# The start of a two-block transformer kernel reordered: smaller first loads, two norms on GpSimd, the context last

## The chip, the cores and the metric

The kernel runs on one core of one Trainium2 chip. The metric is the device time of one execution in microseconds (us). Before the change it is 849.24 us, the median of 3 runs (847.86 to 849.66). The engines are TensorE (PE, with its weight loads as PEld), VectorE (DVE), ScalarE (ACT), GpSimd (POOL) and SyncE (SP), which issues all the DMAs here. Each engine works through its own instructions in a fixed order, and waits on semaphores for the others.

## The reference

The reference runs a first block on `x` (256 tokens of 1024 columns) with a context `ctx` of 256 tokens, and then a second block with a memory `mem` of 256 tokens. What the change touches lies at the first block's start, and in the part of the second block that needs only `mem`:

```python
mod = jax.nn.silu(c) @ w_ada[l] + b_ada[l]            # c: the condition; 6 x 1024 columns
sh1, sc1, gt1, sh2, sc2, gt2 = jnp.split(mod[:, None, :], 6, axis=-1)
mod_c = jax.nn.silu(c_ctx) @ w_ada[l] + b_ada[l]
...
h = modulate(rmsnorm(x, g_norm1[l]), sh1, sc1)         # h * (1 + scale) + shift
hc = modulate(rmsnorm(ctx, g_norm1[l]), shc1, scc1)
cq, ckv, kpe, rq, rk, rv, rg = split_proj(h @ w_in[l])
cq_c, ckv_c, kpe_c, rq_c, rk_c, rv_c, rg_c = split_proj(hc @ w_in[l])
...
m = rms_norm(mem, g_mem[l])                            # second block, cross attention
k = (m @ wk).reshape(B, M, XATTN_HEADS, XATTN_HEAD_DIM)
v = (m @ wv).reshape(B, M, XATTN_HEADS, XATTN_HEAD_DIM)
```

## The kernel before

**Precision.** A weight or an activation is split into a high and a low part in a rounded 32-bit format: ACT makes the high part (`wh`, `xTh`), DVE subtracts it from the source and gets the low part (`wl`, `xTl`). A product is then three matmuls: high by high, high by low, low by high (`mm3`, L185; for the keys of `mem`, `k_step`, L394). So each 512 KB block of weights (a unit) costs one load into one of 7 `raw` buffers, two ACT instructions (L229 where a gain is multiplied in, L222 where not), two DVE instructions (L230, L225) and 12 or 24 matmuls. A `raw` buffer is free again when DVE has read it.

**The start.** `mem`, `x` and `ctx` come transposed (`memT`, `xnT`, `cnT`; `load_T`, L302). `mem_steps` is a list of 16 steps, one unit each: 8 of the keys (`wk_x`, 24 matmuls of 256 columns) and 8 of the values (`wv_x`, 12 matmuls of 512 columns). The modulation rows of the first block need `w_ada`, whose first 2048 columns are 16 loads of 512 KB, used unsplit straight from `raw` (`ada_unit`, L328, 4 matmuls each, into 32-row strips). A string sets in which order the program writes them:

```python
START = 'mmaamxXmaammaammaamaamaakmaaacaC'   # L36
```

Here `m` is a mem step, `a` a unit of `w_ada`, `x` and `c` the loads of `x` and `ctx`, `X` and `C` their norms, `k` a load of constants. After the second `m` the norm of `mem` is written. 11 mem steps stand in the string, the other 5 after the modulation of `x`.

**A norm** (`token_rms`, L354 to L375) squares the transposed tensor on ACT (L357, two instructions of 1024 columns), folds it on DVE (L359, L360, L362: 1024, 512 and 256 columns), sums over partitions with two matmuls against ones (L365), copies the sums to SBUF on DVE (L367), takes the power -0.5 on POOL (L138, L139), spreads the result over the diagonal on DVE (L372) and broadcasts it with one matmul (L374). For `x` and `ctx`, DVE then multiplies (L427).

**After the start.** When the 16 units of `w_ada` are done, `ada_fm` (L343) makes shift and scale, `mod_split` (L468, L471, L159, L160) applies them to `x`, the 5 left mem steps run, and the first projection of `x` begins (four units of `w_in` of 512 columns, 48 matmuls, called the c projection here). The second projection needs `ctx` modulated too (`at<-wh,xTh` are its matmuls on `ctx`).

**What sets the order.** The program is written for a tile framework whose scheduler moves instructions within each engine by priorities (`hp`, `prio`) and by its own costs; the result is one fixed list for each engine. At most 8 DMAs are under way, and a load into `raw` waits for the buffer's last reader.

Of the kernel before, what the change touches and what calls it, by code (L numbers as in the profile page):

```python
# [9 lines left out]
F32 = mybir.dt.float32  # L10
# [4 lines left out]
ALU = mybir.AluOpType  # L15
# [17 lines left out]
MID = 1  # L33
GPU = 3
GPN = 16
START = 'mmaamxXmaammaammaamaamaakmaaacaC'  # L36
NT2 = 3
NS1 = 4
ZORD = ('ka', 'qa', 'qh', 'gh', 'fh', 'ih')
# [50 lines left out]
def _body(nc, tc, A, out, es):  # L90
# [197 lines left out]
    with ExitStack() as e1:  # L288
# [9 lines left out]
        nc.vector.memset(silc, 0.0)  # L298
        C1 = lambda n: c1[:, CST[n][0] - 128:CST[n][1] - 128]

        def load_T(dst, name, q):
            nc.sync.dma_start(dst[:, 4 * q:4 * q + 4, :],  # L302
                              A[name][:, q * 1024:(q + 1) * 1024].rearrange("p (k n) -> p k n", k=4))

        memT = S8()
        wk_units = [units_for(W, A["wk_x"], g * 512, 512, 8, "g_mem") for g in range(2)]
        memT_h = S8(dt=F32R)
        memT_l = S8(dt=F32R)
        load_T(memT, "memT", 0)
        nc.sync.dma_start(fm, A["fm"])  # L310
        for u in wk_units[0][0:HEAD]:
            u.load()
        load_T(memT, "memT", 1)
        nc.sync.dma_start(ident, A["cst1"][:, 0:128])
        for q in range(2):
            ks = slice(4 * q, 4 * q + 4)
            split_from(memT_h[:, ks, :], memT_l[:, ks, :], memT[:, ks, :])
            if q == 0:
                for u in wk_units[0][0:HEADS]:
                    u.get()  # L320
        nc.scalar.activation(silc[:, :, 0:2].rearrange("p k s -> p s k"), fm[:, 0:16].rearrange("p (s k) -> p s k", s=2),
                             AF.Silu)
# [28 lines left out]
        rmem = []  # L351
        rmb = S1()

        def token_rms(xT):  # L354
            sq = [S4() for _ in range(2)]
            for q in range(2):
                nc.scalar.activation(sq[q].rearrange("p (k n) -> p k n", k=4), xT[:, 4 * q:4 * q + 4, :], AF.Square,  # L357
                                     scale=D ** -0.5)
            nc.vector.tensor_tensor(out=sq[0], in0=sq[0], in1=sq[1], op=ALU.add)  # L359
            nc.vector.tensor_tensor(out=sq[0][:, 0:512], in0=sq[0][:, 0:512], in1=sq[0][:, 512:1024], op=ALU.add)  # L360
            s1 = S1()
            nc.vector.tensor_tensor(out=s1, in0=sq[0][:, 0:256], in1=sq[0][:, 256:512], op=ALU.add)  # L362
            t = tr_tile()
            for i in range(2):
                nc.tensor.matmul(t[:, i:i + 1], lhsT=s1[:, i * P:(i + 1) * P], rhs=ones[:, 0:1], start=True, stop=True)  # L365
            ss = small(2, "ss")
            nc.vector.tensor_copy(ss, t[:, 0:2])  # L367
            r = finish_rstd(ss, 2)
            d = S1()
            t = tr_tile()  # L370
            for i in range(2):
                nc.vector.tensor_scalar(out=d[:, i * P:(i + 1) * P], in0=ident, scalar1=r[:, i:i + 1], scalar2=None,  # L372
                                        op0=ALU.mult)
            nc.tensor.matmul(t[:, 0:T], lhsT=ones, rhs=d, start=True, stop=True)  # L374
            return r, t[:, 0:T]  # L375
# [8 lines left out]
        for g in range(2):  # L384
# [17 lines left out]
                                                in1=rmb.unsqueeze(1).broadcast_to([P, 2, T]), op=ALU.mult)  # L402
            for i, u in enumerate(wk_units[g]):
                mem_steps.append(lambda u=u, i=i, f=k_step: f(u, i))
        for g in range(2):
            st = {}

            def v_step(u, i, g=g, st=st):
                if i == 0:
                    st["acc"] = [acc_tile(), acc_tile()]  # L410
                for t in range(2):
                    sl = slice(t * P, (t + 1) * P)
                    gemm_unit([st["acc"][t]], (memT_h[:, :, sl], memT_l[:, :, sl]), u, 8)
                    if i == 3:
                        nc.scalar.activation(vm[t][:, g * 512:(g + 1) * 512], st["acc"][t], AF.Copy, scale=rmem[t])
            for i, u in enumerate(units_for(W, A["wv_x"], g * 512, 512, 8, "g_mem")):
                mem_steps.append(lambda u=u, i=i, f=v_step: f(u, i))

        xnT = S8()
        cnT = S8()  # L420

        @prio("nt")
        def norm_T(dst):
            r, rb = token_rms(dst)
            for q in range(2):
                ks = slice(4 * q, 4 * q + 4)
                nc.vector.tensor_tensor(out=dst[:, ks, :], in0=dst[:, ks, :],  # L427
                                        in1=rb.unsqueeze(1).broadcast_to([P, 4, T]), op=ALU.mult)

        n_mem = n_ada = 0  # L430
        for ch in START:
# [7 lines left out]
                n_ada += 1  # L439
            elif ch == "x":  # L440
                for q in range(2):
                    load_T(xnT, "xT", q)
            elif ch == "c":
                for q in range(2):
                    load_T(cnT, "ctxT", q)
            elif ch == "k":
                nc.sync.dma_start(c1, A["cst1"][:, 128:NC1])
            elif ch == "X":
                norm_T(xnT)
            elif ch == "C":  # L450
# [1079 lines left out]
```

## Time and profile before

| what | value |
|---|---|
| median of the timed runs | 849.24 us |
| the profiled execution | 849.74 us |
| its span (first to last instruction) | 848.0 us |
| PE busy | 815.4 us, 96% |
| DVE busy | 587.6 us, 69% |
| ACT busy | 453.7 us, 54% |
| POOL busy | 50.3 us, 6% |

Times below are counted from the span's start. A busy share is an average over stages; PE's idle time is what is left of the span. In a timeline a row is a run of like instructions: its start, how long it lasted, engine, line, what it writes and reads, how often, and in brackets how long the engine stood idle before it and what ended that. The matmuls' ends are modelled and overlap, so the pace is read from the starts of rows that follow each other.

### The profile page before, as it was taken

How to read it: one execution, taken by the hardware profiler on the slowest of the kernel's cores; microseconds unless marked ns; L12 is line 12 of the kernel's file. 1: busy time of each engine (PE TensorE's matmuls, PEld its weight loads, DVE VectorE, ACT ScalarE, POOL GpSimd, SP SyncE). 2: the span in 40 equal slices, each digit the busy share in tenths (PEclk: the TensorE clock that was granted, in tenths of full speed). 3: DMA queues.
4: the chain of work that ended last, by engine and by line, in shares of the span. 5: the costliest groups of instructions: out<-in, count | busy, mean ns of one | idle time of the engine just before them, and what ended most of it. 6: DMA issues, size and time to landing. Idle time of an engine off the chain costs nothing.

```text
span 848.0 us, 12889 instructions
## 1 busy us (share of the span) xinstructions
PE 815.4 (96%) x4944; PEld 689.1 (81%) x4944; DVE 587.6 (69%) x900; ACT 453.7 (54%) x717; POOL 50.3 (6%) x85
## 2 busy tenths in 40 slices
PE   6989989999999999999999999999999999999996
PEld 5857967666787899999997877777788899999995
DVE  5649879985787697667577767776747855656642
ACT  7348364234556675555455757665626845544531
POOL 0000020111010000000002200101001100000000
PEclk9999999999999999999999999999999999999999
DMA  9797869762155566565664643343624676666501
GB/s 338 271 356 283 280 236 341 253 225 75 50 162 177 188 209 197 176 197 178 196 178 146 184 139 110 138 126 124 198 75 126 196 223 183 190 182 192 176 1 51
DMA packets 65150, 155.27 MB, mean 183 GB/s; under 512 B 5184, under 2 KB 10816, under 8 KB 65088
## 3 DMA queue, kind: packets, MB, share of 16 engines
q1 hardware_dynamic: 65088, 154.44, 56.8%
q8 instruction: 39, 0.64, 0.3%
q14 instruction: 23, 0.19, 0.1%
HBM read 152.85 MB, written 1.05 MB: 181 GB/s over the span
## 4 chain that ended last, share of the span: by engine, by line
PE 67%; ACT 3%; DVE 2%; issue 1%; POOL 1%; DVEq 0%; POOLq 0%; ACTq 0%
PE acc L185 32%; PE at L255 12%; PE tr L255 12%; PE tr L167 1%; PE at L1293 1%; PE at L1271 1%; PE tr L1212 1%; ACT xh L222 1%; DVE xl L225 1%; ACT junk L143 1%; PE at L1162 1%; PE at L1164 1%; PE tr L756 0%; PE at L785 0%; PE at L802 0%
## 5 line engine op out<-in xcount | busy, mean ns | idle before, releaser
L222 ACT CAST wh<-raw 128x1024 fp32r<-128x1024 f32 (+1 forms) x90 | 91.0, 1013 | 103.6 <-PE acc L185 29.4
L225 DVE TENSOR_TENSOR wl<-raw,wh 128x1024 fp32r<-128x1024 f32 (+1 forms) x87 | 104.2, 1200 | 47.5 <-ACT wh L222 46.8
L225 DVE TENSOR_TENSOR xl<-raw,xh 128x1024 fp32r<-128x1024 f32 x68 | 84.4, 1245 | 42.3 <-ACT xh L222 41.9
L185 PE MATMUL acc<-wh,xTh 128*128 128x512 f32 (+2 forms) x272 | 99.8, 392 | 0.3 <-ACT xTh L159 0.3
L222 ACT CAST xh<-raw 128x1024 fp32r<-128x1024 f32 x68 | 70.8, 1047 | 53.5 <-PE tr L255 24.6
L185 PE MATMUL acc<-wl,xTh 128*128 128x512 f32 (+2 forms) x272 | 97.8, 384 | 0.0
L185 PE MATMUL acc<-wh,xTl 128*128 128x512 f32 (+2 forms) x272 | 97.6, 383 | 0.0
L229 ACT ACTIVATE wh<-raw,fm 128x512 fp32r<-128x512 f32 (+3 forms) x96 | 64.0, 712 | 50.7 <-issue 15.6
L230 DVE SCALAR_TENSOR_TENSOR wl<-raw,fm,wh 128x512 fp32r<-128x512 f32 (+3 forms) x96 | 67.2, 742 | 25.6 <-ACT wh L229 25.3
L185 PEld LDWEIGHTS acc<-wh,xTh 128*128 128x128 f32 x272 | 50.6, 190 | 12.2 <-issue 2.1
L185 PEld LDWEIGHTS acc<-wl,xTh 128*128 128x128 f32 x272 | 50.5, 189 | 10.1 <-issue 2.0
L185 PEld LDWEIGHTS acc<-wh,xTl 128*128 128x128 f32 x272 | 50.6, 189 | 9.9 <-issue 1.5
L185 PE MATMUL acc<-xh,xTl 128*128 128x512 f32 x144 | 53.5, 397 | 0.0
L185 PE MATMUL acc<-xl,xTh 128*128 128x512 f32 x144 | 53.3, 396 | 0.2 <-DVE xl L225 0.2
L185 PE MATMUL acc<-xh,xTh 128*128 128x512 f32 x144 | 53.1, 396 | 0.0
L230 DVE SCALAR_TENSOR_TENSOR xl<-raw,fm,xh 128x512 fp32r<-128x512 f32 (+1 forms) x44 | 33.3, 796 | 17.8 <-ACT xh L229 17.7
L185 PE MATMUL acc<-xh,g 128*128 128x512 f32 x160 | 44.5, 391 | 0.0
L229 ACT ACTIVATE xh<-raw,fm 128x512 fp32r<-128x512 f32 (+1 forms) x44 | 31.1, 756 | 22.5 <-issue 13.0
L539 DVE SCALAR_TENSOR_TENSOR g<-raw,silc,g 128x1024 f32<-128x1024 f32 x28 | 36.8, 1313 | 0.1
L185 PE MATMUL acc<-wh,g 128*128 128x512 f32 x128 | 36.3, 390 | 0.0
L185 PEld LDWEIGHTS acc<-xh,g 128*128 128x128 f32 x160 | 29.6, 188 | 5.8
L185 PEld LDWEIGHTS acc<-xl,xTh 128*128 128x128 f32 x144 | 26.7, 188 | 6.4 <-DVE xl L225 1.1
(381 smaller groups left out, 1736.1 us busy)
## 6 DMA issues: line engine op xcount, KB each, us to landing
raw<-in_w_up_dram SPq DMA_DIRECT2D x66, 512.0 KB, 3.8
raw<-in_w_ada_dram SPq DMA_DIRECT2D x48, 512.0 KB, 5.6
raw<-in_w_down_dram SPq DMA_DIRECT2D x44, 512.0 KB, 3.6
raw<-in_w_in_dram SPq DMA_DIRECT2D x38, 512.0 KB, 4.0
raw<-in_w_gate_dram SPq DMA_DIRECT2D x22, 512.0 KB, 3.7
raw<-in_w_out_dram SPq DMA_DIRECT2D x16, 512.0 KB, 3.5
raw<-in_wk_x_dram SPq DMA_DIRECT2D x8, 512.0 KB, 5.8
raw<-in_wv_x_dram SPq DMA_DIRECT2D x8, 512.0 KB, 8.2
```

The costliest lines, as they stand in the source:

```text
L143: nc.scalar.activation(junk[:, 0:a.shape[-1]], a, AF.Square, scale=n ** -0.5, accum_out=ss)
L167: nc.tensor.transpose(t[:, j * P:(j + 1) * P], src[:, (b + j) * P:(b + j + 1) * P], ident)
L185: nc.tensor.matmul(accs[i], lhsT=xl if f == 2 else xh, rhs=wl[i] if f == 1 else wh[i], start=first and f == 0, stop=last and f == 2)
L222: nc.scalar.copy(wh[:, 0:n], raw[:, 0:n])
L225: eng.tensor_tensor(out=wl[:, 0:n], in0=raw[:, 0:n], in1=wh[:, 0:n].bitcast(F32), op=ALU.subtract)
L229: nc.scalar.activation(wh[:, s], raw[:, s], AF.Copy, scale=gains[k])
L230: nc.vector.scalar_tensor_tensor(out=wl[:, s], in0=raw[:, s], scalar=gains[k], in1=wh[:, s].bitcast(F32), op0=ALU.mult, op1=ALU.subtract)
L255: nc.tensor.matmul(accs[b // 2][:, (b % 2) * T:(b % 2 + 1) * T], lhsT=wt[:, o:o + P], rhs=xt[:, k, :], start=k == 0 and fl == 0 and b % 2 ...
L539: nc.vector.scalar_tensor_tensor(out=ada_cur[g], in0=raw, scalar=silc[:, k, 0:1], in1=ada_cur[g], op0=ALU.mult, op1=ALU.add)
L1162: nc.tensor.matmul(o[cs, hs], lhsT=ATs[cs, cols], rhs=ih[cs, hs], start=True, stop=cg == 0)
L1164: nc.tensor.matmul(o[cs, hs], lhsT=qi[:, cols], rhs=Sst[cg - 1][:, hs], start=False, stop=True)
L1212: nc.tensor.matmul(sc[:, j * nk:(j + 1) * nk], lhsT=qTs[pr_, hd * P:(hd + 1) * P], rhs=kTs[pr_, 0:nk], start=True, stop=True)
```

## The change

- `fm`, a tensor of small columns with the condition in it, is loaded first, and the Silu of the condition is ACT's first work. The first half of `memT` and the first unit of `wk_x` are loaded in two pieces each, alternately; `memT` is split in three pieces.
- The norms of `mem` and `x` are squared and folded on POOL (`early=True`). The norm of `ctx` squares on ACT and folds on DVE as before. The factor 1/1024 moves from the squares to the copy of the sums.
- `START` has 12 mem steps ahead of the last units of `w_ada` (11 before; 4 are left for after the modulation), and the norm of `x` has priority there. `L` loads the units of `wv_x` that are left, and then `ctx`; the norm of `ctx` is written after the last mem step.
- The two columns `lb0`, `lb1` of the second block get a load of their own, late.

```diff
-START = 'mmaamxXmaammaammaamaamaakmaaacaC'
+START = 'mmaamxXaammaamaammaamkaammaamaaL'
...
-        def load_T(dst, name, q):
-            nc.sync.dma_start(dst[:, 4 * q:4 * q + 4, :],
-                              A[name][:, q * 1024:(q + 1) * 1024].rearrange("p (k n) -> p k n", k=4))
+        def load_T(dst, name, k0, nk=4):
+            nc.sync.dma_start(dst[:, k0:k0 + nk, :],
+                              A[name][:, k0 * T:(k0 + nk) * T].rearrange("p (k n) -> p k n", k=nk))
...
-        load_T(memT, "memT", 0)
         nc.sync.dma_start(fm, A["fm"])
-        for u in wk_units[0][0:HEAD]:
-            u.load()
-        load_T(memT, "memT", 1)
-        nc.sync.dma_start(ident, A["cst1"][:, 0:128])
-        for q in range(2):
-            ks = slice(4 * q, 4 * q + 4)
-            split_from(memT_h[:, ks, :], memT_l[:, ks, :], memT[:, ks, :])
-            if q == 0:
-                for u in wk_units[0][0:HEADS]:
-                    u.get()
         nc.scalar.activation(silc[:, :, 0:2].rearrange("p k s -> p s k"), fm[:, 0:16].rearrange("p (s k) -> p s k", s=2),
                              AF.Silu)
+        u0 = wk_units[0][0]
+        u0.raw = W().raw()
+        for k in range(2):
+            load_T(memT, "memT", 2 * k, 2)
+            nc.sync.dma_start(u0.raw[:, k * 512:(k + 1) * 512], u0.ap[k * P:(k + 1) * P, :])
+        load_T(memT, "memT", 4)
+        wk_units[0][1].load()
+        nc.sync.dma_start(ident, A["cst1"][:, 0:128])
+        for k0, nk in ((0, 2), (2, 2), (4, 4)):
+            ks = slice(k0, k0 + nk)
+            split_from(memT_h[:, ks, :], memT_l[:, ks, :], memT[:, ks, :])
+            if k0 == 0:
+                u0.get()
+            if k0 == 2:
+                wk_units[0][1].get()
...
-        def token_rms(xT):
+        def token_rms(xT, early=True):
             sq = [S4() for _ in range(2)]
+            eng = nc.gpsimd if early else nc.vector
             for q in range(2):
-                nc.scalar.activation(sq[q].rearrange("p (k n) -> p k n", k=4), xT[:, 4 * q:4 * q + 4, :], AF.Square,
-                                     scale=D ** -0.5)
-            nc.vector.tensor_tensor(out=sq[0], in0=sq[0], in1=sq[1], op=ALU.add)
-            nc.vector.tensor_tensor(out=sq[0][:, 0:512], in0=sq[0][:, 0:512], in1=sq[0][:, 512:1024], op=ALU.add)
+                xq = xT[:, 4 * q:4 * q + 4, :]
+                sv = sq[q].rearrange("p (k n) -> p k n", k=4)
+                if early:
+                    nc.gpsimd.tensor_tensor(out=sv, in0=xq, in1=xq, op=ALU.mult)
+                else:
+                    nc.scalar.activation(sv, xq, AF.Square)
+            eng.tensor_tensor(out=sq[0], in0=sq[0], in1=sq[1], op=ALU.add)
+            eng.tensor_tensor(out=sq[0][:, 0:512], in0=sq[0][:, 0:512], in1=sq[0][:, 512:1024], op=ALU.add)
             s1 = S1()
-            nc.vector.tensor_tensor(out=s1, in0=sq[0][:, 0:256], in1=sq[0][:, 256:512], op=ALU.add)
+            eng.tensor_tensor(out=s1, in0=sq[0][:, 0:256], in1=sq[0][:, 256:512], op=ALU.add)
...
-            nc.vector.tensor_copy(ss, t[:, 0:2])
+            nc.vector.tensor_scalar(out=ss, in0=t[:, 0:2], scalar1=1.0 / D, scalar2=None, op0=ALU.mult)
...
-            elif ch == "c":
+            elif ch == "L":
+                for i in range(n_mem, 16):
+                    wv_units[(i - 8) // 4][i % 4].load()
                 for q in range(2):
-                    load_T(cnT, "ctxT", q)
+                    load_T(cnT, "ctxT", 4 * q)
...
             elif ch == "X":
-                norm_T(xnT)
-            elif ch == "C":
-                norm_T(cnT)
+                with hp("nt"):
+                    norm_T(xnT)
...
             mem_steps[i]()
+        norm_T(cnT, False)
```

The scheduler puts the moved work into each engine's list. First POOL, from its first norm on. In the names here and below, `s_94` is `memT`, `s_95` and `s_96` are its high and low part, `s_125` (before) or `s_129` (after) is `xnT`, `s_126` or `s_130` is `cnT`, and `g_181`, `g_182`, `g_251`, `g_252` are squares. Before:

```order
L138 TENSOR_SCALAR rs_190<-ss_188 128x2 [waits DVE_49]
L139 TENSOR_TENSOR rs_190<-rs_190,mhalf 128x2 [waits Pool_49]
L138 TENSOR_SCALAR rs_260<-ss_258 128x2 [waits DVE_49]
L139 TENSOR_TENSOR rs_260<-rs_260,mhalf 128x2 [waits Pool_49]
L138 TENSOR_SCALAR rs_598<-ss_596 128x2 [waits DVE_49]
```

And now:

```order
L365 TENSOR_TENSOR g_181<-s_94 128x1024 [waits DMAHW3_49,DMAHW1_49]
L365 TENSOR_TENSOR g_182<-s_94 128x1024 [waits DMAHW5_49]
L368 TENSOR_TENSOR g_181<-g_181,g_182 128x1024 [waits Pool_49]
L369 TENSOR_TENSOR g_181<-g_181 128x512 [waits Pool_49]
L371 TENSOR_TENSOR s1k<-g_181 128x256 [waits Pool_49]
L138 TENSOR_SCALAR rs_194<-ss_192 128x2 [waits DVE_49]
L139 TENSOR_TENSOR rs_194<-rs_194,mhalf 128x2 [waits Pool_49]
L365 TENSOR_TENSOR g_251<-s_129 128x1024 [waits DMAHW3_49]
L365 TENSOR_TENSOR g_252<-s_129 128x1024 [waits DMAHW4_49]
L368 TENSOR_TENSOR g_251<-g_251,g_252 128x1024 [waits Pool_49]
L369 TENSOR_TENSOR g_251<-g_251 128x512 [waits Pool_49]
L371 TENSOR_TENSOR s1k<-g_251 128x256 [waits Pool_49]
```

Five wide instructions stand ahead of each of the first two powers, and those of `x` stand behind `mem`'s power.

Second PE, around `mem`'s sum over partitions (L365 before, L374 now) and its broadcast (L374 before, L383 now); `at<-raw,silc` are the units of `w_ada`. Before:

```order
L394 MATMUL acc<-s_95,wl 128x256 [waits DVE_49]
L394 MATMUL acc<-s_95,wl 128x256 x3
L365 MATMUL tr<-ones,s1k 128x1 [waits DVE_49]
L365 MATMUL tr<-ones,s1k 128x1
L328 MATMUL at<-raw,silc 32x256 x3
L328 MATMUL at<-raw,silc 32x256 [waits DMAHW7_49]
L328 MATMUL at<-raw,silc 32x256 x3
L394 MATMUL acc<-s_95,wh 128x256 [waits Activation_49]
L394 MATMUL acc<-s_95,wh 128x256 x3
L394 MATMUL acc<-s_96,wh 128x256 x4
L394 MATMUL acc<-s_95,wl 128x256 [waits DVE_49]
L374 MATMUL tr<-s1k,ones 128x256 [waits DVE_49]
```

And now:

```order
L403 MATMUL acc<-s_95,wl 128x256 [waits DVE_49]
L403 MATMUL acc<-s_95,wl 128x256 x3
L374 MATMUL tr<-ones,s1k 128x1 [waits Pool_49]
L374 MATMUL tr<-ones,s1k 128x1
L332 MATMUL at<-raw,silc 32x256 [waits DMAHW0_49]
L332 MATMUL at<-raw,silc 32x256 x3
L332 MATMUL at<-raw,silc 32x256 [waits DMAHW1_49]
L332 MATMUL at<-raw,silc 32x256 x3
L383 MATMUL tr<-s1k,ones 128x256 [waits DVE_49]
L403 MATMUL acc<-s_95,wh 128x256 [waits Activation_49]
L403 MATMUL acc<-s_95,wh 128x256 x3
L403 MATMUL acc<-s_96,wh 128x256 x4
```

The sum now waits for POOL, and between the sum and the broadcast there are two units of `w_ada` where there were these and half a mem step. The norm of `x` follows in the same shape: one mem step, one unit of `w_ada`, its sum, one unit of `w_ada`, its broadcast, the next mem steps.

Third DVE, from the last `wl` of the mem steps to the splits of `ctx`. Before:

```order
L230 SCALAR_TENSOR_TENSOR wl<-raw,fm,wh 128x512 x4
L487 TENSOR_SCALAR lg<-lg 128x8
L225 TENSOR_TENSOR wl<-raw,wh 128x1024
L489 TENSOR_SCALAR nlb<-lg 128x4
L493 TENSOR_SCALAR wst<-lg,c_91 128x4 x4
L225 TENSOR_TENSOR wl<-raw,wh 128x1024
L471 TENSOR_SCALAR s_126<-s_126,sc_609,sh_608 128x256 x5
L225 TENSOR_TENSOR wl<-raw,wh 128x1024 x2
L160 TENSOR_TENSOR xTl<-s_126,xTh 128x1024 x2
```

And now:

```order
L230 SCALAR_TENSOR_TENSOR wl<-raw,fm,wh 128x512 x4
L368 TENSOR_TENSOR g_727<-g_727,g_728 128x1024
L369 TENSOR_TENSOR g_727<-g_727 128x512
L499 TENSOR_SCALAR lg<-lg 128x8
L371 TENSOR_TENSOR s1k<-g_727 128x256
L501 TENSOR_SCALAR nlb<-lg 128x4
L505 TENSOR_SCALAR wst<-lg,c_91 128x4 x4
L376 TENSOR_SCALAR ss_738<-tr 128x2
L225 TENSOR_TENSOR wl<-raw,wh 128x1024
L381 TENSOR_SCALAR s1k<-ident,rs_740 128x128 x2
L225 TENSOR_TENSOR wl<-raw,wh 128x1024
L437 TENSOR_TENSOR s_130<-s_130,tr 128x1024 x2
```

The whole norm of `ctx` stands among the low parts of the c projection's weights now (L225; the modulation and the splits of `ctx` follow, with the third and fourth L225 between and behind them); before, it stood ahead of the modulation of `x`.

## Rows read from the trace of the kernel before

**Rows 1.** The page, first part: busy time, share of the span, instructions.
```profile
PE 815.4 (96%) x4944; PEld 689.1 (81%) x4944; DVE 587.6 (69%) x900; ACT 453.7 (54%) x717; POOL 50.3 (6%) x85
```
**Rows 2.** Timeline, PE at the start: start us, lasted us, instructions.
```profile
7.90 2.08 PE L394 MATMUL acc<-s,wh 128*128 128x256 f32 x8 [7.90 <-ACT wh L229]
...
17.19 0.50 PE L365 MATMUL tr<-ones,s1k 128*128 128x1 f32 x4
...
37.19 1.21 PE L394 MATMUL acc<-s,wh 128*128 128x256 f32 x8
...
43.13 1.07 PE L328 MATMUL at<-raw,silc 128*32 128x256 f32 x16
44.13 0.50 PE L185 MATMUL acc<-wh,s 128*128 128x512 f32 x1
...
47.07 1.07 PE L328 MATMUL at<-raw,silc 128*32 128x256 f32 x16
```
**Rows 3.** Busy time of each engine and granted clock in three stretches of the start.
```profile
core 0: us, PE busy (x) PEld busy (x) DVE busy (x) ACT busy (x) POOL busy (x), PEclk, DMA share, GB/s
7.90:13.00 5.10, 5.10 (x24) 5.10 (x24) 2.75 (x4) 5.07 (x7) 0.00 (x0) 1.00 1.04 409
54.70:60.80 6.10, 3.32 (x39) 1.58 (x38) 2.74 (x5) 3.11 (x4) 0.15 (x1) 1.00 1.03 360
60.80:64.20 3.40, 3.23 (x9) 1.75 (x8) 1.84 (x5) 2.82 (x6) 1.30 (x2) 0.50 0.98 359
```
**Rows 4.** Timeline, PE: last units of `w_ada`, and the end of the c projection.
```profile
58.06 0.64 PE L328 MATMUL at<-raw,silc 128*32 128x256 f32 x8 [1.51 <-DMA raw<-in_w_ada_dram]
...
89.83 0.39 PE L185 MATMUL acc<-wh,xTl 128*128 128x512 f32 x1
90.05 0.41 PE L185 MATMUL acc<-wh,xTh 128*128 128x256 f32 x2
```
**Rows 5.** Timeline, ACT and DVE at the start.
```profile
0.72 1.28 ACT L159 ACT_TABLE_LOAD   x1 [0.72 <-PEq L1520]
5.11 1.04 ACT L159 CAST s<-s 128x1024 fp32r<-128x1024 f32 x1 [3.10 <-DMA s<-in_memT_dram]
7.13 1.34 ACT L229 ACTIVATE wh<-raw,fm 128x512 fp32r<-128x512 f32 x2 [0.98 <-DMA raw<-in_wk_x_dram]
```
**Rows 6.** DMA issues from 24.5 to 28 us: size, us from issue to landing.
```profile
raw<-in_wk_x_dram SPq DMA_DIRECT2D x1, 512.0 KB, 3.7
```
**Rows 7.** POOL's wide instructions, grouped by shape: busy us, mean ns of one.
```profile
L225 POOL TENSOR_TENSOR wl<-raw,wh 128x1024 fp32r<-128x1024 f32 x3 | 7.2, 2386 | 88.3 <-ACT wh L222 34.4 <-PE tr L745 29.1 <-DVE g L539 24.7
L1316 POOL TENSOR_TENSOR g<-g,bc 128x1024 f32<-128x1024 f32 x1 | 2.6, 2632 | 172.7 <-DMA g<-in_rows_dram 172.7
```
**Rows 8.** DVE's instructions, grouped by shape, first 130 us.
```profile
L230 DVE SCALAR_TENSOR_TENSOR wl<-raw,fm,wh 128x512 fp32r<-128x512 f32 x32 | 22.6, 747 | 9.0 <-ACT wh L229 9.0
L225 DVE TENSOR_TENSOR wl<-raw,wh 128x1024 fp32r<-128x1024 f32 x6 | 7.2, 1218 | 1.4 <-ACT wh L222 1.4
```
**Rows 9.** Timelines, POOL and DVE where both had wide instructions.
```profile
151.21 2.39 POOL L225 TENSOR_TENSOR wl<-raw,wh 128x1024 fp32r<-128x1024 f32 x1 [34.44 <-ACT wh L222]
...
151.35 3.33 DVE L225 TENSOR_TENSOR wl<-raw,wh 128x1024 fp32r<-128x1024 f32 x1
...
451.29 2.63 POOL L1316 TENSOR_TENSOR g<-g,bc 128x1024 f32<-128x1024 f32 x1 [172.71 <-DMA g<-in_rows_dram]
...
452.13 2.87 DVE L225 TENSOR_TENSOR xl<-raw,xh 128x1024 fp32r<-128x1024 f32 x1 [0.47 <-ACT xh L222]
```
**Rows 10.** Timeline, from the sum over partitions to the broadcast, norm of `mem`.
```profile
17.73 0.16 DVE L367 COPY ss<-tr 128x2 f32<-128x2 f32 x1 [0.76 <-PE tr L365]
18.74 0.72 POOL L139 TENSOR_TENSOR rs<-rs,mhalf 128x2 f32<-128x2 f32 x1
20.02 0.70 PE L374 MATMUL tr<-s1k,ones 128*128 128x256 f32 x2
```
**Rows 11.** Busy time of each engine from 59.7 to 82.9 us, columns as above.
```profile
59.70:82.90 23.20, 21.46 (x87) 16.16 (x88) 20.94 (x45) 20.34 (x32) 1.45 (x2) 0.93 0.83 295
```

More of the change, by code (lines that the diff above doesn't have):

```diff
@@ L404, in _body @@
                 mem_steps.append(lambda u=u, i=i, f=k_step: f(u, i))
+        wv_units = {}
         for g in range(2):
@@ L415, in v_step @@
                         nc.scalar.activation(vm[t][:, g * 512:(g + 1) * 512], st["acc"][t], AF.Copy, scale=rmem[t])
-            for i, u in enumerate(units_for(W, A["wv_x"], g * 512, 512, 8, "g_mem")):
+            wv_units[g] = units_for(W, A["wv_x"], g * 512, 512, 8, "g_mem")
+            for i, u in enumerate(wv_units[g]):
                 mem_steps.append(lambda u=u, i=i, f=v_step: f(u, i))
@@ L420, in _body, with norm_T @@
         cnT = S8()
-        @prio("nt")
-        def norm_T(dst):
-            r, rb = token_rms(dst)
+        def norm_T(dst, early=True):
+            r, rb = token_rms(dst, early)
             for q in range(2):
@@ L441, in _body @@
                 for q in range(2):
-                    load_T(xnT, "xT", q)
-            elif ch == "c":
+                    load_T(xnT, "xT", 4 * q)
+            elif ch == "L":
+                for i in range(n_mem, 16):
+                    wv_units[(i - 8) // 4][i % 4].load()
                 for q in range(2):
-                    load_T(cnT, "ctxT", q)
+                    load_T(cnT, "ctxT", 4 * q)
             elif ch == "k":
@@ L1032, in _body @@
     lbd = cp.tile([P, 8], F32, name="lbd")
-    l0, l1 = FM("lb0"), FM("lb1")
+    lbt = s2.tile([P, 8], F32, name="lbt")
+    nc.sync.dma_start(lbt, A["fm"][:, FM_COLS["lb0"][0]:FM_COLS["lb1"][1]])
+    l0, l1 = lbt[:, 0:4], lbt[:, 4:8]
     lmx = cp.tile([P, 4], F32, name="lmx")
```

## The prediction

> **What bounds the kernel now.** I read the page first: PE is busy 815.4 us of the 848.0 us span [rows 1], so 32.6 us are idle, and everything else can only matter through PE. The page's slices show where that idle time is: PE starts late, it dips between 50 and 70 us, and behind that it is near full. So I read PE's timeline of the start next [rows 2]. PE stands until 7.90 us. Then 24 matmuls of 256 columns take 5.10 us [rows 3], at 0.21 us each, while two mem steps of the same kind take 5.94 us for 48 (37.19 to 43.13) [rows 2], 0.124 us each: by its pace PE begins at the lower of its two clocks, 1.2 of 2.4 GHz, for 5.1 us, though the clock's column reads 1.00 there. From 13 to 55 us PE hardly waits. Between 54.70 and 60.80 us it is busy 3.32 us of 6.10, waiting for the last units of w_ada and then for the norm of ctx, and from 60.80 to 64.20 us the granted clock is 0.50 behind that [rows 3]. The reader is to see that the start costs PE roughly 20 us beyond its work, and that the start ends where the c projection ends, 90.05 us [rows 4]. Behind that PE is the bound again, so what the change wins or loses up to there is what the kernel wins or loses. The changed order has six narrower matmuls drawn ahead of that end; with the four that PE really has done more there (0.5 us) my mark is 90.55 us.
>
> **First matmul.** Now fm (138 KB by its shape) comes first and the table load waits for it. A lone load of 512 KB takes 3.7 us [rows 6], so a smaller one that is issued at 0.72 us is there by 4.4 us; I take 3.6 us. Table load 1.28 us, Silu 0.2 us, half a cast 0.55 us, first high part 0.67 us [rows 5] give 6.3 us instead of 7.90, bounds 5.7 and 7.1. That is the gain: 1.6 us.
>
> **The norm of mem.** Its three wide steps run on POOL, where 1024 columns took 2.39 and 2.63 us [rows 7]; with 2.5 us, and 1.25 and 0.65 us for the two narrower folds, the chain is 9.4 us. It can begin when the first half of memT is there, about 6.2 us. But it does not run alone. Where POOL had begun at 151.21 us, DVE's subtraction of two tensors in SBUF took 3.33 us instead of 1.22, and at 452.13 us 2.87 us [rows 9, 8]: both times it ended one own duration after POOL's instruction (151.21+2.39+1.22 is 154.82, and it ended at 154.68). So DVE is stopped for the rest of POOL's instruction. The splits of memT and of the first units, seven DVE instructions (0.65, 0.75, 0.65, 0.75, 1.2, 0.75, 0.75 us by size) [rows 8], lie exactly beside POOL's five. No row shows what happens when a stopped DVE instruction and POOL's next one both stand ready. I take turns: DVE goes in between each time. POOL's last fold then ends at 6.2 + 9.4 + four or five of DVE's (3.7 us), 19.3 us, DVE's last wl at 20.5 us, and PE, which needs each wl before it may go on, finishes its second mem step and reaches mem's sum at 21 us. Before it was there at 17.19 us [rows 2]. If POOL held on through all five, DVE would wait some 9 us once; mem's sum would come at 21 us too, and the next norm 1.3 us later. Without the stops it would be 16 us. The Trainium skill ("SBUF — State Buffer", section "Who interferes with whom") says that such a pair shares a port that whoever issues first holds for the whole instruction. The trace agrees with the holding; by that rule the turns that I take are what comes, and the sum stays; no row here shows the turns.
>
> **The norm of x.** POOL takes it up behind mem's power. From mem's sum (0.5 us) to the power's end took 17.73 to 19.46 us before [rows 10], so 23 us now; the chain of 9.4 us with DVE's two wl and the diagonal in between (2.0 us) ends at 34.4 us. x's broadcast follows 2.4 us behind its sum (17.73 to 20.02 [rows 10], less what the first call of the power cost), at 36.8 us; then DVE multiplies x (2.3 us) before it may make the next wl (0.75 us), as its order has it: 40.3 us. Between mem's sum and x's broadcast PE's order has four units of w_ada, one mem step and the norms' own matmuls, 6 us of work in 16 us: PE stands for some 10 us in pieces. 36 of the two mem steps' 48 matmuls stand behind that, 4.5 us: 44.8 us.
>
> **To the last unit of w_ada.** From there PE's order holds six pairs of units (1.0 us, 43.13 to 44.13), three mem steps of keys (2.97 us each) and four of values (2.94 us each, 44.13 to 47.07) [rows 2]: 26.7 us, less 0.3 us where steps follow directly, so 26.4 us: 71.2 us, against 58.7 us before [rows 4]. The loads don't lengthen that: walking the buffers, each unit of w_ada lands some 5 us before PE asks, since a lone load takes 3.7 us [rows 6] and its buffer was freed some 12 us earlier. That the order has one mem step more ahead of this point saves nothing by itself; it is PE work either way.
>
> **To the end of the c projection.** The norm of ctx was done early, while DVE had nothing else; now its folds (1.2, 0.7, 0.4 us by size [rows 8]) stand among DVE's fullest stretch. Before, DVE was busy 20.94 of the 23.20 us that end with the fourth low part of the c projection's weights [rows 11]. Now that is 20.94, less two low parts (0.75 us each), plus 2.3 us: 21.7 us, with 2.3 us of waits as before and 1.3 us from the last unit to DVE's first instruction: 25.3 us. Ten matmuls follow (2.2 us, 0.22 each by 89.83 to 90.05 [rows 4]): 27.5 us. PE's own work in it is 96 wide matmuls and 2 us of small ones, 23.5 us, so it stands 4 us. If DVE hid all of that, 23.5 us is the lower bound.
>
> **Sum.** 71.2 + 27.5 is 98.7 us, against 90.55: 8.1 us later. Against the profiled execution's own 849.74 us this is 857.8 us; that execution lies 0.5 us above the median of the runs shown, so on the median's footing 857.3 us. Small edits: the load of lb0 and lb1, a table load that moves behind the start and one more in the feed-forward part (1.28 us on ACT, which is far from full) I put at nothing, hidden by PE's matmuls; uncovered they cost 1.3 us. ACT loses four squares (4 us) in the start, which gives nothing while PE waits for POOL and DVE.
>
> The Trainium skill's page "GPSIMD Engine Reference", section "Elementwise — side-by-side cycle accounting", gives 4497 ns for an add of 2048 columns; an estimate from it is 2.25 us for 1024, which is below both rows here. By it each chain is 8.4 us and the sum 2 us lower, 855.3 us.
>
> **Rivals.** *No stops.* POOL and DVE run side by side, and the two long overlaps that I found mislead. Then mem's sum is at 16 us, x's at 28 us, the last unit of w_ada at 64.8 us, and the mark at 92.3 us: 851.0 us. That both came out to within 0.15 us speaks against it [rows 9]. *DVE's late stretch is hidden.* The chain to the last unit is as forecast, but PE works through at 23.5 us: 853.3 us. *Faster, through POOL's squares.* A square reads one tensor, not two, and no row shows that. If POOL's wide instructions took what DVE's take (1.22 us, [rows 8]), mem's sum would wait for nobody, x's sum would be at 21 us, the last unit at 57.2 us, the mark at 84.7 us: 843.4 us. The point from which this decides is about 1.5 us for 1024 columns with the stops and 2.1 us without; the two rows lie above both. *A lower clock.* PE's work between 10 and 40 us is thin, and the clock halved behind a thin stretch of 6 us before [rows 3]. Most of that hides in the waits; 36 matmuls at 0.21 instead of 0.124 us would add 3 us: 860.4 us.
>
> **How the numbers follow.** Forecast with the lower clock as its upper part 0.67, hidden late stretch 0.08, no stops 0.14, faster through POOL 0.11. Of the case without stops 0.05 falls within 0.2% (1.7 us, about what a measurement can tell from no change) and 0.02 below it. So faster 0.13, same 0.05, slower 0.82. The likeliest time is 857.3 us; 8 in 10 lie between 850.5 us (no stops) and 864 us (the lower clock, POOL holding through and the uncovered loads on top: 857.3 + 3 + 1.3 + 1.3 is 862.9 us, and 1 us for the first load).
>
> **What would show it.** In the changed profile: first matmul near 6.3 us; POOL's squares of 1024 columns at 2.4 us or longer; DVE's first splits and low parts stretched to 2 to 3 us; PE waiting for POOL at both sums, at about 21 and 34 us; the last unit of w_ada near 71 us; the c projection's end near 99 us, and from there the same distance to the end as before. I am wrong if POOL's chain ends before PE comes to the sum, if DVE's low parts beside it keep their 0.75 us, or if the part behind 100 us changes its length by more than 1.5 us.

## The result, and the profile after

The changed kernel takes 856.16 us, the median of 4 runs (855.72 to 859.87), against 849.16 us for the kernel before beside it: a ratio of 1.0082, 95% interval 1.0063 to 1.0100. It is slower by 7.0 us; 857.3 us was forecast. Its profiled execution took 856.07 us, with a span of 854.3 us.

First the page of the changed kernel (busy time, share of the span, instructions), to be held against [rows 1]:

```profile
PE 815.7 (95%) x4944; PEld 689.1 (81%) x4944; DVE 595.0 (70%) x895; ACT 451.2 (53%) x715; POOL 69.1 (8%) x95
```

PE's work is the same to 0.3 us. The span grew by 6.3 us, so PE's idle time grew from 32.6 to 38.6 us. POOL has 18.8 us more.

PE's timeline of the changed kernel (start, lasted, instruction, count, idle time before and what ended it), against [rows 2, 4]:

```profile
7.18 2.07 PE L403 MATMUL acc<-s,wh 128*128 128x256 f32 x8 [7.18 <-ACT wh L229]
...
16.52 1.23 PE L403 MATMUL acc<-s,wl 128*128 128x256 f32 x4 [2.36 <-DVE wl L230]
...
19.84 0.50 PE L374 MATMUL tr<-ones,s1k 128*128 128x1 f32 x4
...
25.52 1.22 PE L383 MATMUL tr<-s1k,ones 128*128 128x256 f32 x2 [4.18 <-DVE s1k L381]
...
31.68 0.61 PE L374 MATMUL tr<-ones,s1k 128*128 128x1 f32 x4
...
34.19 0.70 PE L383 MATMUL tr<-s1k,ones 128*128 128x256 f32 x2 [1.33 <-DVE s1k L381]
...
37.99 0.74 PE L403 MATMUL acc<-s,wl 128*128 128x256 f32 x4 [1.69 <-DVE wl L230]
...
42.49 1.07 PE L332 MATMUL at<-raw,silc 128*32 128x256 f32 x16
...
68.54 1.07 PE L332 MATMUL at<-raw,silc 128*32 128x256 f32 x16
...
98.58 0.41 PE L185 MATMUL acc<-wl,xTh 128*128 128x256 f32 x2
```

The brackets tell the story: 2.36 us for a low part from DVE, then 4.18 us for the diagonal of mem's norm, which is two tiny DVE instructions; behind that 1.33 us for x's diagonal and 1.69 us for a low part. At neither sum (L374, 19.84 and 31.68 us) does PE wait for POOL. The last unit of w_ada ends near 69.5 us (58.7 before), the c projection at 98.58 us (90.55 before): 8.0 us later.

Why DVE was late stands in two timelines of the changed kernel side by side, POOL first:

```profile
7.23 2.43 POOL L365 TENSOR_TENSOR g<-s 128x1024 f32<-128x1024 f32 x1 [6.80 <-DMA s<-in_memT_dram]
10.67 1.96 POOL L365 TENSOR_TENSOR g<-s 128x1024 f32<-128x1024 f32 x1 [1.00 <-DMA s<-in_memT_dram]
12.71 3.21 POOL L368 TENSOR_TENSOR g<-g,g 128x1024 f32<-128x1024 f32 x1
15.99 1.61 POOL L369 TENSOR_TENSOR g<-g 128x512 f32<-128x512 f32 x1
17.68 1.06 POOL L371 TENSOR_TENSOR s1k<-g 128x256 f32<-128x256 f32 x1
...
21.64 3.75 POOL L365 TENSOR_TENSOR g<-s 128x1024 f32<-128x1024 f32 x2
25.46 2.36 POOL L368 TENSOR_TENSOR g<-g,g 128x1024 f32<-128x1024 f32 x1
...
29.58 1.07 POOL L371 TENSOR_TENSOR s1k<-g 128x256 f32<-128x256 f32 x1
```

and DVE:

```profile
7.83 2.38 DVE L160 TENSOR_TENSOR s<-s,s 128x512 fp32r<-128x512 f32 x1
...
11.70 2.01 DVE L160 TENSOR_TENSOR s<-s,s 128x1024 fp32r<-128x1024 f32 x1 [0.82 <-ACT s L159]
13.63 4.51 DVE L230 SCALAR_TENSOR_TENSOR wl<-raw,fm,wh 128x512 fp32r<-128x512 f32 x2
...
21.70 3.76 DVE L381 TENSOR_SCALAR s1k<-ident,rs 128x128 f32<-128x128 f32 x2 [1.17 <-POOL rs L139]
```

The two low parts at 13.63 us take 4.51 us; alone they take 1.5 us [rows 8]. The diagonal starts 0.06 us behind POOL's squares of x and is done when both squares are, one instruction behind each square: 3.76 us for work that takes 0.48 us where POOL is quiet (x's, at 33.65 us). That POOL had just given DVE the power it waited for, and went straight on to the squares, is what put the two side by side.

The clock in four stretches of the changed kernel (columns as in [rows 3]: length, busy time and instructions of each engine, granted clock, DMA share, GB/s):

```profile
core 0: us, PE busy (x) PEld busy (x) DVE busy (x) ACT busy (x) POOL busy (x), PEclk, DMA share, GB/s
16.08:19.50 3.42, 2.98 (x14) 2.98 (x15) 2.07 (x2) 1.33 (x2) 2.58 (x2) 0.50 1.02 402
22.91:29.74 6.83, 4.22 (x16) 3.77 (x17) 5.59 (x6) 2.51 (x4) 6.59 (x5) 0.50 0.37 140
69.54:98.58 29.04, 25.82 (x115) 19.46 (x111) 26.75 (x51) 22.55 (x34) 1.85 (x2) 1.00 0.77 270
123.67:127.09 3.42, 3.42 (x21) 2.46 (x22) 2.98 (x12) 3.12 (x8) 1.10 (x3) 1.00 0.37 147
```

and the kernel before, in the stretch with the work that the changed kernel does at 123.67 us:

```profile
115.41:118.83 3.42, 3.42 (x12) 2.75 (x13) 2.75 (x11) 2.57 (x7) 1.19 (x3) 0.50 0.04 15
```

The changed kernel spent 10.2 us of its start at the lower clock (0.50, the level of 1.2 GHz); the kernel before had 3.4 us there [rows 3] and another 3.4 us at 115 us, which the changed one has not. These are single executions, and e1 below has that later stretch too.

### The profile page after: what moved, and what is told of

Read it like the earlier page. It is cut to its first block, busy times and chain, and to the rows that moved or that the text cites. A ratio compares the mean times of both kernels' runs of the same rounds, so it can differ in the third digit from the quotient of the medians.

```text
span 854.3 us, 12899 instructions
## 1 busy us (share of the span) xinstructions
PE 815.7 (95%) x4944; PEld 689.1 (81%) x4944; DVE 595.0 (70%) x895; ACT 451.2 (53%) x715; POOL 69.1 (8%) x95
## 4 chain that ended last, share of the span: by engine, by line
PE 65%; ACT 4%; DVE 3%; issue 1%; POOL 1%; DVEq 0%; POOLq 0%; ACTq 0%
PE acc L185 31%; PE at L255 12%; PE tr L255 12%; PE tr L167 1%; PE at L1307 1%; PE at L1285 1%; PE tr L1226 1%; DVE xl L225 1%; ACT xh L222 1%; ACT junk L143 1%; PE at L1176 1%; PE at L1178 1%; PE tr L768 0%; PE at L797 0%; PE at L814 0%
## 5 line engine op out<-in xcount | busy, mean ns | idle before, releaser
L225 DVE TENSOR_TENSOR wl<-raw,wh 128x1024 fp32r<-128x1024 f32 (+1 forms) x87 | 101.9, 1175 | 44.8 <-ACT wh L222 44.1
L225 DVE TENSOR_TENSOR xl<-raw,xh 128x1024 fp32r<-128x1024 f32 x68 | 84.9, 1253 | 41.3 <-ACT xh L222 41.0
L230 DVE SCALAR_TENSOR_TENSOR wl<-raw,fm,wh 128x512 fp32r<-128x512 f32 (+3 forms) x96 | 71.8, 790 | 23.6 <-ACT wh L229 23.2
L551 DVE SCALAR_TENSOR_TENSOR g<-raw,silc,g 128x1024 f32<-128x1024 f32 x28 | 39.8, 1420 | 0.1
```

The costliest lines, as they stand in the source:

```text
L225: eng.tensor_tensor(out=wl[:, 0:n], in0=raw[:, 0:n], in1=wh[:, 0:n].bitcast(F32), op=ALU.subtract)
L230: nc.vector.scalar_tensor_tensor(out=wl[:, s], in0=raw[:, s], scalar=gains[k], in1=wh[:, s].bitcast(F32), op0=ALU.mult, op1=ALU.subtract)
L551: nc.vector.scalar_tensor_tensor(out=ada_cur[g], in0=raw, scalar=silc[:, k, 0:1], in1=ada_cur[g], op0=ALU.mult, op1=ALU.add)
```

## The experiments

Ratios are to the kernel before, on the same chip, with 95% intervals; us are the ratio less one, times the 850.2 to 850.7 us that it took there (849.2 us beside the changed kernel).

| kernel | POOL makes | ratio | us |
|---|---|---|---|
| changed | norms of mem and x | 1.0082 (1.0063 to 1.0100) | +7.0 |
| e1 | none | 0.9969 (0.9957 to 0.9981) | -2.6 |
| e3 | mem's norm | 1.0019 (1.0004 to 1.0034) | +1.6 |
| e7 | x's norm | 1.0027 (1.0014 to 1.0041) | +2.3 |
| e2 (from before) | both norms | 1.0107 (1.0090 to 1.0124) | +9.1 |
| e4 | both; ctx early | 1.0083 (1.0063 to 1.0104) | +7.1 |
| e6 | both; diagonals on ACT | 1.0072 (1.0057 to 1.0088) | +6.1 |
| e5 (from before) | 5 unused instructions | 1.0069 (1.0050 to 1.0088) | +5.9 |
| e9 (from before) | 2 unused, at mem's power | 1.0053 (1.0039 to 1.0067) | +4.5 |
| e10 (from before) | 2 unused, at 31 us | 1.0016 (1.0005 to 1.0027) | +1.4 |
| e8 | none; old loads | 0.9978 (0.9968 to 0.9988) | -1.9 |
| e14 | none; norms written later | 1.0009 (0.9994 to 1.0023) | +0.8 |
| e15 | e14 with old loads | 1.0021 (1.0007 to 1.0034) | +1.8 |

**Which part of the change costs: e1, e2, e4.** My theory was that POOL's norms cost nearly all; the rival, the new order with ctx last.

From the changed kernel to e1:

```diff
-            r, rb = token_rms(memT)
+            r, rb = token_rms(memT, False)
...
-                    norm_T(xnT)
+                    norm_T(xnT, False)
```

> The changed kernel, but with the norms of mem and x squared on ACT and folded on DVE, as before. Theory (the two norms on POOL cost nearly all of the 7.0 us): the sums come some 3 and 7 us sooner, mem's near 17 us and x's near 25 us, no wait of 4 us for the diagonal; PE's waits for the late norm of ctx (3.1 us between 69.5 and 98.6 us in the changed kernel) stay, but the wait of 2.8 us and the lower clock (1.7 us) that the early norm of ctx had go, and the first matmul is 0.7 us sooner: 847 to 849.5 us against 849.2 us of before. Rival (the late norm of ctx and the new order cost it): 853 us or more.

Measured: 847.06 us against 850.21. Two of PE's waits in e1, grouped (total us, times, longest):

```profile
PE tr L383 <- DVE s1k L381: 3.0, 3, 1.3
...
PE acc L403 <- DVE wl L230: 0.6, 1, 0.6
```

In the changed kernel these groups hold 6.3 and 4.0 us. Without the two `gpsimd` norms the rest of the change is a gain of 2.6 us, and no other kernel here has a lower ratio (e8 comes close, and the intervals overlap). The two norms on POOL cost 9.6 us (1.0082 less 0.9969). The two profiled spans, 854.3 and 847.4 us, differ by 6.9 us; e1's profiled execution, 849.14 us, is among the slowest of its twelve.

From the kernel before to e2, which takes over only `token_rms` (for `ctx` with `early=False`):

```diff
-                nc.scalar.activation(sq[q].rearrange("p (k n) -> p k n", k=4), xT[:, 4 * q:4 * q + 4, :], AF.Square,
-                                     scale=D ** -0.5)
...
+                    nc.gpsimd.tensor_tensor(out=sv, in0=xq, in1=xq, op=ALU.mult)
...
-            nc.vector.tensor_tensor(out=sq[0], in0=sq[0], in1=sq[1], op=ALU.add)
+            eng.tensor_tensor(out=sq[0], in0=sq[0], in1=sq[1], op=ALU.add)
```

From the changed kernel to e4, where `c` and `C` are again the load and the norm of `ctx`:

```diff
-START = 'mmaamxXaammaamaammaamkaammaamaaL'
+START = 'mmaamxXaammaamaammaamkaammaacmaaCL'
```

> The kernel before, but with the norms of mem and x on POOL; its loads, its order of steps and its early norm of ctx stay. Theory (POOL's norms are the price): x's broadcast comes some 8 us later than before, 855 to 858 us. Rival (order and late norm of ctx): at most 851 us.

> The changed kernel, but with the load of ctx and its norm (ACT and DVE) ahead of the last four units of w_ada, as before. Theory (place of ctx's norm is about neutral: it ends 3.1 us of waits late in the stretch and brings back a wait of some 2.8 us, perhaps with 1.7 us of lower clock): 855 to 858 us, against 856.2 us of the changed kernel. Rival (the late norm costs what the prediction put it at, 4 us): 852 to 853 us.

e2 came out just above its range, e4 inside its own. POOL's norms put on the old kernel alone cost 9.1 us; where ctx is normed is, with the norms on POOL, worth nothing that these runs can tell (e4's interval is 1.8 us to either side). No run has ctx early without POOL's norms.

**mem or x: e3, e7.** Each takes one of e1's two lines alone.

> The changed kernel with only the norm of x back on ACT and DVE; mem's stays on POOL. With neither on POOL the ratio to before was 0.997, with both 1.008. Theory (mem's part is the smaller: its sum comes 1.5 us later, with some lower clock behind it; the diagonal meets no POOL work): 1.001 to 1.0035. Rival (the early splits are where the loss lies): 1.0045 or more.

> The changed kernel with only the norm of mem back on ACT and DVE; x's stays on POOL, where its squares again follow mem's power and lie beside the diagonal. Theory (x's part is the larger: the diagonal stopped for 3.8 us, a lower clock behind that wait, and the long chain): 1.004 to 1.0065. Rival: 1.002 or less.

Over e1, mem's norm on POOL costs 0.0050 (4.2 us) and x's 0.0058 (4.9 us); together 9.2 us, where both cost 9.6. So they add up, and neither is the small one: e3 lies in the range that I gave it, e7 below its own. The profiles show a different stop in each: in e3 PE waits 0.81 and 2.05 us for two low parts and 0.20 us for mem's diagonal, in e7 for no low part ahead of mem's sum and 4.19 us for the diagonal.

**Length of POOL's chain, or DVE's stops: e5, e9, e10, e6.** POOL work that nobody waits for has no chain; what it costs are the stops. The sequences of PE and DVE in the start are those of the kernel before.

From the kernel before to e5; e9 is without the first call of `spare`:

```diff
+        def spare(xT, add):
+            sq = [S4() for _ in range(2)]
+            for q in range(2):
+                xq = xT[:, 4 * q:4 * q + 4, :]
+                nc.gpsimd.tensor_tensor(out=sq[q].rearrange("p (k n) -> p k n", k=4), in0=xq, in1=xq, op=ALU.mult)
+            if add:
+                nc.gpsimd.tensor_tensor(out=sq[0], in0=sq[0], in1=sq[1], op=ALU.add)
...
             r, rb = token_rms(memT)
+            spare(memT, True)
...
                 norm_T(xnT)
+                spare(memT, False)
```

> The kernel before, with POOL work added that nobody waits for: two squares and an add of 1024 columns on memT beside the first splits, two more squares behind mem's power. Orders of PE and DVE stay as before. First theory (the length of POOL's own chain is the price; DVE's stops beside it are small change): DVE's first low parts stretch to 2 to 3 us, mem's sum comes at most 1.5 us later, 849 to 851 us. Rival (the stops of DVE are the price, whoever makes the norm): 853 us or more.

> The kernel before with only two squares of 1024 columns added on POOL, behind the power of mem's norm, that nobody waits for. Theory (one stop in the wrong place is most of it): the diagonal takes 3.8 instead of 0.5 us, mem's broadcast comes 3.3 us later and all behind it, 1.003 to 1.005 of before. Rival (the loss lay with the first splits): at most 1 us, under 1.0015.

My first theory of e5 fell: unused POOL work alone cost 5.9 us. e9, just above the range of its theory, shows where most of that is. POOL, DVE and PE in e9, then its clock in two stretches:

```profile
19.40 3.74 POOL L381 TENSOR_TENSOR g<-s 128x1024 f32<-128x1024 f32 x2
```
```profile
19.46 3.76 DVE L372 TENSOR_SCALAR s1k<-ident,rs 128x128 f32<-128x128 f32 x2 [0.93 <-POOL rs L139]
```
```profile
23.28 1.22 PE L374 MATMUL tr<-s1k,ones 128*128 128x256 f32 x2 [3.36 <-DVE s1k L372]
...
24.93 1.91 PE L402 MATMUL acc<-s,wh 128*128 128x256 f32 x8
26.64 1.05 PE L402 MATMUL acc<-s,wl 128*128 128x256 f32 x4
...
30.34 0.50 PE L365 MATMUL tr<-ones,s1k 128*128 128x1 f32 x4
```
```profile
17.16:22.45 5.29, 2.76 (x29) 1.95 (x27) 3.82 (x4) 3.40 (x6) 4.41 (x4) 1.00 1.03 396
22.45:29.27 6.82, 5.99 (x25) 5.65 (x25) 5.41 (x9) 2.01 (x4) 0.69 (x1) 0.50 0.43 142
```

One stop makes PE wait 3.36 us. While it waits, the granted clock falls to 0.50 and stays there to 29.27 us, and the eight matmuls at 24.93 us take 1.71 us. In the kernel before the same eight took 0.96 us, and x's sum came at 24.41 us:

```profile
20.91 1.12 PE L394 MATMUL acc<-s,wh 128*128 128x256 f32 x8
21.87 0.64 PE L394 MATMUL acc<-s,wl 128*128 128x256 f32 x4
...
24.41 0.50 PE L365 MATMUL tr<-ones,s1k 128*128 128x1 f32 x4
```

So x's sum is 5.9 us later: 3.3 us for the later broadcast, and 2.7 us for the pace behind it. Up to x's sum the stop cost 1.8 times its 3.3 us; over the whole run e9 lost 4.5 us. In e5 PE waits the same 3.36 us, the granted clock is 0.50 for 3.4 us only (25.48 to 28.89), and the pace behind the broadcast costs 1.5 us.

> The same two squares of 1024 columns on POOL, but reading the first keys, so that they run from about 33 us, where DVE only makes low parts with time to spare. Theory (it is the place, not the work): within 0.1% of before, though one or two low parts are stopped. Rival (each POOL instruction beside DVE costs its length): 2 us or more, 1.0025 or more.

The same two squares reading `kTm[0]` ran from 30.92 us. The eight low parts beside them in e10 took 8.66 us together; in the kernel before they took 5.38 us:

```profile
30.76 8.66 DVE L230 SCALAR_TENSOR_TENSOR wl<-raw,fm,wh 128x512 fp32r<-128x512 f32 x8
```
```profile
33.85 0.74 PE L402 MATMUL acc<-s,wl 128*128 128x256 f32 x4 [0.61 <-DVE wl L230]
...
36.15 0.74 PE L402 MATMUL acc<-s,wl 128*128 128x256 f32 x4 [0.61 <-DVE wl L230]
```

The kernel lost 1.4 us, between my two theories: the place matters by a factor of three, but the slack was smaller than I thought. PE waits for two of these low parts (second fence), where before it waited for neither, and goes from 0.3 us behind the kernel before (31.55 us against 31.21) to 2.0 us behind (38.25 against 36.20). Later it waits 2.41 us for a load of w_ada at 61.00 us, which was 1.51 us at 58.06 us before [rows 4]; that this comes from a low part that freed its `raw` buffer late is argued, not shown.

From the changed kernel to e6, in `token_rms` where `early` is set:

```diff
-                nc.vector.tensor_scalar(out=d[:, i * P:(i + 1) * P], in0=ident, scalar1=r[:, i:i + 1], scalar2=None,
-                                        op0=ALU.mult)
+                nc.scalar.activation(d[:, i * P:(i + 1) * P], ident, AF.Copy, scale=r[:, i:i + 1])
```

> The changed kernel with the two small diagonals of the norms of mem and x on ACT, not DVE; POOL's norms stay. First theory (POOL's own chain for x is the bound behind mem's sum): mem's broadcast comes 3.3 us sooner, x's sum hardly sooner; at most 1 us won, 1.007 to 1.0085 of before. Rival (the 3.8 us in which the diagonal is stopped are the price there): 3 us won, 1.0045 to 1.006 of before.

e6 lies with the first theory: at most 1 us won, within what the runs can tell. ACT made the diagonal in 0.69 us beside POOL's squares. Mem's sum came at 21.41 us in that execution, 1.6 us later than in the changed kernel; counted from there, the broadcast came 2.7 us sooner and x's sum 0.6 us, because PE then met POOL itself:

```profile
32.63 0.61 PE L374 MATMUL tr<-ones,s1k 128*128 128x1 f32 x4 [0.64 <-POOL s1k L371]
```

So both hold: in the changed kernel the stops lie on the path, and where one is taken off, POOL's chain of 9 us behind it is nearly as late.

**The first loads, and a try for the best: e8, e14, e15.**

From e1 to e8, and from e14 to e15, the first loads, the splits and the Silu go back to what they were before:

```diff
+        load_T(memT, "memT", 0)
         nc.sync.dma_start(fm, A["fm"])
...
-        for k in range(2):
-            load_T(memT, "memT", 2 * k, 2)
-            nc.sync.dma_start(u0.raw[:, k * 512:(k + 1) * 512], u0.ap[k * P:(k + 1) * P, :])
+        for u in wk_units[0][0:HEAD]:
+            u.load()
         load_T(memT, "memT", 4)
```

From e1 to e14:

```diff
-START = 'mmaamxXaammaamaammaamkaammaamaaL'
+START = 'mmaamxaammaamaaXmmaamkaammaamaaL'
-                if n_mem == 2:
+                if n_mem == 3:
                     mem_norm()
...
-                with hp("nt"):
-                    norm_T(xnT, False)
+                norm_T(xnT, False)
```

> The kernel of the first experiment (norms of mem and x on ACT and DVE, norm of ctx late, 12 mem steps first) with the first loads and the Silu as before. First theory (smaller pieces cost more than they give: with them the second unit of wk_x landed at 12.3 us, before at 10.0 us, and mem's sum came at 18.3 us, before at 17.2 us): about 1 us under that kernel, 0.995 to 0.9965 of before. Rival (the first matmul, 1.7 us sooner with small pieces, is a lasting gain): 0.7 to 1.7 us over that kernel, 0.9975 to 0.999 of before.

> A try for the best: the kernel of the first experiment (no wide POOL work), with the norm of mem written behind the third mem step and that of x behind some more, so that PE meets the broadcasts later. Theory: the waits of 0.9 and 1.3 us for the diagonals shrink, 0.995 to 0.9965 of before. Rival (DVE's next low parts are late in their place): as without it, 0.9965 to 0.998.

> The same as the other kernel of this call without wide POOL work, with the first loads and the Silu as before the change. First theory (smaller pieces cost at the mark: with the old loads the second projection's end was at 108.7 us, not 110.3 us, and a lower clock behind it hid that): 1 to 1.5 us under that kernel. Rival (the small pieces give a lasting gain): 0.8 us or more over it.

Both pairs fall on the rival's side: with the old loads e8 is 0.0009 over e1, and e15 0.0012 over e14. The intervals of each pair overlap, so about 1 us for the smaller pieces is likely, not shown, and it isn't seen at the end of the c projection: there e8 is 1.5 us ahead of e1 (90.08 us against 91.61), e15 1.0 us behind e14. A part may lie at the very end: from the start of the last matmul to the span's end the seven profiled kernels with the new loads take 6.8 to 7.1 us, the seven with the old ones 7.3 to 7.5 us. Why is not shown. e14 is a miss. It was to hide the waits for the broadcasts, but in its sequence x's sum comes close behind mem's broadcast, and PE waits for both of x's steps:

```profile
26.23 0.58 PE L374 MATMUL tr<-ones,s1k 128*128 128x1 f32 x4 [1.93 <-DVE s1k L371]
...
28.71 1.22 PE L383 MATMUL tr<-s1k,ones 128*128 128x256 f32 x2 [1.90 <-DVE s1k L381]
```

These rows explain a part at most: at the end of the c projection e14's profile is 1.1 us behind e1's, and the ratios differ by 3.4 us. e1 stays the best version here; it and e8 beat both kernels.

## Why the prediction was right

Half of the mechanism was the one forecast: POOL's wide instructions stop DVE, PE waits for what DVE makes, and the start is longer. The other half failed, that PE would wait for POOL at both sums. POOL's chains ended at 18.74 and 30.65 us, and PE came to the sums 1.1 and 1.0 us after that, held up by DVE (2.36 us for the low part, 4.18 us for the diagonal) and by the lower clock. That POOL's chain ends before PE comes to the sum was one of the signs by which I called myself wrong. The size at the mark was right to 0.1 us (98.58 against 98.7), and that is luck: terms that were off by -2.3, +0.6 and +1.5 us cancel.

- **First matmul.** Forecast 6.3 us with bounds of 5.7 and 7.1; it came at 7.18 us, just outside. The step that failed is that fm's landing sets it. ACT in the changed kernel had done the Silu by 4.55 us, and then stood 0.82 us for the 256 KB piece of wk_x:

```profile
4.32 0.23 ACT L310 ACTIVATE silc<-fm 128x16 f32<-128x16 f32 x1
...
6.41 0.72 ACT L229 ACTIVATE wh<-raw,fm 128x512 fp32r<-128x512 f32 x1 [0.82 <-DMA raw<-in_wk_x_dram]
```

  The seven kernels with these loads have their first matmul between 6.18 us (e1) and 7.44 us (e4, e6), so one execution fixes this term to a microsecond at best.
- **Norm of mem.** Sum forecast at 21 us, measured 19.84; DVE's last low part was done at 18.15 us (forecast 20.5). DVE and POOL did take turns: DVE's part goes in when POOL's instruction ends, and POOL's add at 12.71 us took 3.21 us, its like at 25.46 us 2.36 us. The Trainium skill ("SBUF — State Buffer", "Who interferes with whom") has DVE instructions with two SBUF inputs contending with GpSimd's reads, and counts copies and tensor_scalar among those that can. This case agrees with both kinds: the low parts and the diagonal were stopped.
- **Norm of x.** All its steps came 2.3 to 2.7 us sooner than forecast: broadcast 34.19 (36.8), first low part 37.99 (40.3), next w_ada unit 42.49 (44.8). The mis-sized term is POOL's chain: I took 2.5 us for a wide step from [rows 7], and a square took 1.9 us (3.75 for two); and DVE's pieces did not lengthen it by the 2.0 us that I added. The chain ran from 21.64 to 30.65 us, 9.0 us.
- **To the last unit of w_ada.** Forecast 26.4 us, measured 27.0 (42.49 to 69.5).
- **To the end of the c projection.** Forecast 27.5 us, measured 29.0. PE was busy 25.8 us of it, 2.3 us more than I counted, and stood 3.2 us. That it would be hidden (23.5 us) fell.
- **Behind the mark.** I forecast the same distance to the end, and called myself wrong if it changed by more than 1.5 us. It shrank by 1.7 us (757.4 to 755.7), so this step failed. It is tempting to put that down to the lower clock at 115 us, which is gone in the changed kernel, but e1 has it and the same short distance: its c projection ends at 91.61 us, 755.8 us before the end of its span (e1's mark and clock):

```profile
91.61 0.41 PE L185 MATMUL acc<-wl,xTh 128*128 128x256 f32 x2
```
```profile
115.58:119.00 3.42, 3.05 (x11) 2.48 (x12) 2.17 (x11) 2.03 (x7) 1.58 (x4) 0.50 0.68 264
```

  The last matmul starts 6.9 us later than before (first the kernel before, then the changed one), and the other 0.6 us lies behind it, as in all kernels with the new loads. What made the 1.1 us between the mark and the last matmul stays open.

```profile
840.51 0.39 PE L185 MATMUL acc<-wh,g 128*128 128x512 f32 x1
```
```profile
847.43 0.39 PE L185 MATMUL acc<-wh,g 128*128 128x512 f32 x1
```

- **Rivals.** *No stops* fell at the DVE rows. *Faster through POOL's squares* had its point right in kind, since squares are quicker than adds, but 1.9 us lies above the 1.5 us from which it decides. *A lower clock* came, for 10.2 us in the start, but not where I had priced it: the 36 matmuls behind x's broadcast ran at a granted clock of 1.00 (34.54 to 42.49 us). What the 10.2 us cost is not shown.

What I did not see is the worth of the rest of the change. I counted the early loads as the gain of 1.6 us and ctx's late norm as a loss of 4 us of standing. e1 has all of that and is 2.6 us faster than before, and POOL's norms cost 9.6 us, more than the 7.0 us that the whole change lost. Where e1's gain lies is not shown. Its profiled execution ends the c projection 1.1 us later than the kernel before (91.61 us against 90.55) and its span is only 0.6 us shorter, so the gain isn't one of the start there; its faster executions were not profiled.

## What to carry to other kernels

POOL is not a free engine while DVE makes what PE waits for: price each wide POOL instruction as a stop of whatever DVE has beside it, the tiny instruction on the critical path above all. Look at what POOL does right after it hands DVE a result, because here that is where the two collided. Where PE stands some 3 us and goes on at half clock, price the wait above its length: here, up to the next sum, at 1.5 times (e5) and 1.8 times (e9).

## What the hardware showed that I had not expected

- A DVE instruction's size does not limit its stop. In e5 a `tensor_tensor` of 4 columns beside POOL's square took 1.55 us; the next one of that shape took 0.16 us:

```profile
5.61 1.55 DVE L1045 TENSOR_TENSOR lmx<-fm 128x4 f32<-128x4 f32 x1 [4.33 <-DMA fm<-in_fm_dram]
7.20 0.16 DVE L1046 TENSOR_TENSOR lbd<-fm,lmx 128x4 f32<-128x4 f32 x1
```

- The turns are strict, and so the number of DVE's instructions counts. The row of the two diagonals looks as if they were held over both squares (3.76 us over 3.75), but each was held over one. In the changed kernel the first diagonal ended at 23.61 us, 0.07 us behind the first square, and the second pair (POOL, then DVE) is

```profile
23.49 1.89 POOL L365 TENSOR_TENSOR g<-s 128x1024 f32<-128x1024 f32 x1
```
```profile
23.54 1.93 DVE L381 TENSOR_SCALAR s1k<-ident,rs 128x128 f32<-128x128 f32 x1
```

  The two low parts at 13.63 us likewise ended 0.6 us behind POOL's add and 0.6 us behind its next fold. In none of the runs does a DVE instruction of the first 50 us stay stopped past the end of one wide POOL instruction. Whether one diagonal of 256 columns would have been stopped only once was not run.
- A POOL square that reads one tensor took 1.9 us for 1024 columns, an add of two 2.36 us.
